# Stick-breaking attention by parts: one sigmoid, running products times differences of neighbouring value rows, with the value rows kept in DRAM

## The chip, the core and the metric

One core of a Trainium2 chip runs the whole kernel as one launch. The metric is the device time of one launch in microseconds (us); the time before is the median of three runs. A separate execution was taken by the hardware profiler, and all durations below come from it. The engines are PE (TensorE, matrix products), DVE (VectorE), ACT (ScalarE), POOL (GpSimd, which also issues DMAs from its own queue) and SP (which issues most loads).

## The reference, cut to what matters

The kernel computes one layer of a hybrid block for 1024 tokens of width 1024: a norm, one input projection, stick-breaking attention (8 heads of width 64), a gated linear recurrence (4 heads of width 128), gates, an output projection, an MLP and a last norm. The change touches only the attention:

```python
z = jnp.einsum('bhqd,bhkd->bhqk', qi, k) * scale
mask = kpos[None, :] < qpos[:, None]
log_beta = jax.nn.log_sigmoid(z)
log_rem = jnp.where(mask, log_beta - z, 0.0)
between = lax.cumsum(log_rem, axis=3, reverse=True) - log_rem
w = jnp.where(mask, jnp.exp(log_beta + between), 0.0)
return jnp.einsum('bhqk,bhkd->bhqd', w, v)
```

For a query t and a key s < t the weight is sigmoid(z_ts) times the product of sigmoid(-z_tj) over the keys j between s and t. Write R_s for the product of sigmoid(-z_tj) over s <= j < t, with R_t = 1. Because sigmoid(z) = 1 - sigmoid(-z), the weight equals R_(s+1) - R_s. Summation by parts then gives sum_s w_s v_s = sum_s (R_s - 1)(v_(s-1) - v_s), with a zero row in the place of v_(-1).

## The kernel before, in words

All matrix products are made in a split form: an operand is stored as a rounded part ("hi", type fp32r) and the remainder ("lo"). `hi_lo` (lines 152 to 154) makes both: a copy on ACT (line 144) writes hi, a subtraction on DVE (line 149) writes lo. A projection is then three matmuls per tile (`three`, line 526, all recorded at line 121).

The work is written out as one order by hand. There are two lanes of PE work (`open_block`, line 103): "main" holds the attention's own steps, "fill" holds projection steps that a `Stream` (`st`, line 471) hands out in small portions, so that PE has something to do while the other engines work on the attention. Jobs of the stream are, in order: the Q and K columns of each head (`qk_item`, line 676) and the V columns of four heads at once, a "quad" (`v_job`, line 670); behind them come projections for the recurrence. The first job (`first_job`, line 703) holds head 0's Q and K and the V columns of quad 0. The V columns of quad 1 (`v_job(1)`, line 729) stand behind head 4's Q and K. Instructions of one engine run in the order in which they stand in its queue; the tile framework places them, and lines with `after(...)` fix the order of some.

The attention is a list of 64 items (line 732): for each head the query blocks 7, 0, 6, 1, 5, 2, 4, 3 of 128 queries. The loop at line 2136 does for item i: `weights` of item i+1, `scores` of item i+2, some fill steps, `turn` of item i, and at times `values`.

- `scores` (line 736): two matmuls per 512 keys into a PSUM bank `z` (QH and QL against KS), then two sigmoids on ACT: `rm` = sigmoid(-z/8), stored one place to the left (line 755), and `bt` = sigmoid(z/8) (line 758). POOL clears the last column of `bt` (line 759).
- `weights` (line 767): a running product over `rm` from the right on DVE (line 777), which is set to 1 where the byte mask `bits` has a 1, and a product of `bt` and `rm` on DVE (line 787, recorded at line 157), 72 of each.
- `turn` (line 791): PE transposes `bt` in blocks of 128 x 128 into a bank `pw` (line 823), and `hi_lo` writes it as `wTh` and `wTl`. For an even query block POOL clears the block of keys that it doesn't reach (line 811).
- `values` (line 831): for a pair of query blocks, matmuls `po` with the V tile of each key block as weights and `wTh`, `wTl` as moving operand; ACT and DVE add the two halves of `po` into `osb` (lines 850 and 851). It runs one item behind the second `turn` of the pair.

The V tiles are made by `v_epilogue` (line 636): from a PSUM bank with 128 tokens of a quad, `hi_lo` writes hi and lo of each head side by side. `v_stat` (line 648) picks head and key block. The Q and K epilogue (line 652) writes QH, QL and KS and lets POOL issue two SBUF copies (line 663). Between them POOL issues one-time sums of output weights in DRAM (`out_weight_sums`, line 1205, issues at line 1213, tile `tw`).

On-chip buffers come from a pool of 40 full tiles of 128 x 1024 (`slot`) and 10 halves of 128 x 512 (`slot_n` up to 512 columns, `half`).

Of the kernel before, what the change touches and what calls it, by code (L numbers as in the profile page):

```python
# [19 lines left out]
P = 128  # L20
T = 1024
# [18 lines left out]
def kernel(  # L40
# [34 lines left out]
    def slot(name, dt=F32):  # L75
        return spool.tile([P, 1024], dt, tag="s", name=name)

    def slot_n(name, n, dt=F32):

        if n <= 512:  # L80
            return hpool.tile([P, 512], dt, tag="h", name=name)
        return slot(name, dt)

    def bank(name):
        return psum.tile([P, 512], F32, tag="p", name=name)
# [545 lines left out]
            )  # L631


    vt, qk, osb = {}, {}, {}

    def v_epilogue(quad):


        def ep(ps, tb):
            if tb % 2 == 0:  # L640
                vt[quad, tb // 2] = slot(f"V{quad}_{tb // 2}", F32R)
            V = vt[quad, tb // 2].rearrange("p (t h s d) -> p t h s d", t=2, h=4, s=2)
            src = ps.rearrange("p (h d) -> p h d", h=4)
            hi_lo(V[:, tb % 2, :, 0, :], V[:, tb % 2, :, 1, :], src)

        return ep

    def v_stat(h, tb):
        c = ((tb % 2) * 4 + h % 4) * P
        return vt[h // 4, tb // 2][:, c : c + P]  # L650

    def qk_epilogue(h):
        def ep(ps, half):
# [71 lines left out]
    j_qk = {0: j_first}  # L725
    for h in range(1, NHS):
        j_qk[h] = proj_jobs([qk_item(h)], xn)
        if h == 4:
            v_job(1)

    QB_ORDER = (7, 0, 6, 1, 5, 2, 4, 3)
    items = [(h, qb) for h in range(NHS) for qb in QB_ORDER]
# [3 lines left out]
    def scores(h, qb):  # L736
        open_block("main")
        nk = (qb + 1) * P
        QH, QL, KS = qk[h]
        bt, rm = slot_n(f"bt{h}_{qb}", nk), slot_n(f"rm{h}_{qb}", nk)  # L740
        step = 320 if nk == 640 else 512
        for s0 in range(0, nk, step):
            m = min(nk - s0, step)
            n = max(m, 256)
            z = bank(f"z{h}_{qb}_{s0}")
            for i, Q in enumerate((QH, QL)):
                matmul(
                    z[:, :n],
                    Q[:, qb * P : (qb + 1) * P],
                    KS[:, s0 : s0 + n],  # L750
                    start=i == 0,
                    stop=i == 1,
                )
            c0, e = int(s0 == 0), m - (s0 + m == nk)
            nc.scalar.activation(  # L755
                rm[:, s0 + c0 - 1 : s0 + m - 1], z[:, c0:m], AF.Sigmoid, scale=-0.125
            )
            nc.scalar.activation(bt[:, s0 : s0 + e], z[:, :e], AF.Sigmoid, scale=0.125)  # L758
        lastsel[0] = nc.gpsimd.memset(bt[:, nk - 1 : nk], 0.0)
        zs[h, qb] = (bt, rm)  # L760


    bits = cpool.tile([P, 1024], U8, tag="bits", name="bits")
    nc.gpsimd.memset(bits, 0)
    nc.vector.tensor_copy(bits[:, 1024 - P - 1 : 1023], ident)

    def weights(h, qb):

        nk = (qb + 1) * P
        bt, rm = zs[h, qb]
        cut = qb == NT - 1
        parts = ((512, nk - 1), (0, 512)) if cut else ((0, nk - 1),)
        for i, (a, b) in enumerate(parts):
            rr = rm[:, a:b][:, ::-1]
            sc = nc.vector.tensor_tensor_scan(  # L777
                out=rr,
                data0=rr,
                data1=bits[:, 1024 - nk + a : 1024 - nk + b][:, ::-1],  # L780
                initial=rm[:, b : b + 1] if i else 0.0,
                op0=ALU.mult,
                op1=ALU.max,
            )
            if i == 1 or (qb == 5 and h in (2,)):
                after(sc, turn_lo[0])
            m = mul(bt[:, a:b], bt[:, a:b], rm[:, a:b])
            if qb == 5:
                after(m, turn_lo[0])

    def turn(h, qb, between):

        open_block("main")
        bt, rm = zs.pop((h, qb))
# [12 lines left out]
        tiles = wTt[h, qc]  # L807
        qs = slice(par * P, (par + 1) * P)
        if par == 0:
            for t in tiles[-1]:  # L810
                after(nc.gpsimd.memset(t[:, (nkb - 1) % 4, qs].bitcast(F32), 0.0), lastsel[0])
# [341 lines left out]
    class Split:  # L1153
# [15 lines left out]

    a_sb, a_hg = Split("asb"), Split("ahg")  # L1170
    mgs = Acts("ms")
    scratch = ctx.enter_context(
        tc.tile_pool(name="scratch", bufs=1, space=bass.MemoryType.DRAM)
    )

    def dram(name, shape):
        return scratch.tile(shape, F32, tag=name, name=name)

    def half(name, dt=F32):
        return hpool.tile([P, 512], dt, tag="h", name=name)  # L1180

    def add(out, a, b):
        return nc.vector.tensor_tensor(out=out, in0=a, in1=b, op=ALU.add)

# [1102 lines left out]
```

## Time and profile before

| What | Value |
|---|---|
| time, median of 3 runs | 1452.63 us (1452.25 to 1452.66) |
| profiled execution: span from the first to the last instruction | 1450.9 us |
| the profiled execution's own time | the page gives the span only; 1.7 us lie between it and the median |
| attention in the trace | first scores at 50.11 us, last value product near 315.5 us |
| TENSOR_TENSOR_SCAN at line 777 | 72, 87.3 us in all on DVE |
| QH and QL copies issued by POOL at line 663 | 16 each, 128 KB each, 2.2 us from issue to landing |
| granted clock of PE, mean | 0.997 |

A row of a group in the profile gives the line, the engine, the operation, what it writes and reads, the count, then the busy time in us and the mean of one in ns, then the idle time of the engine just before these instructions with what ended it. A row of the windows view gives a stretch, its length, and the busy time and number of instructions of PE, of PE's weight loads (PEld), DVE, ACT and POOL, the granted clock, the busy share of the DMA engines and what they moved. In a row of the timeline the first two numbers are the start and the duration in us.

### The profile page before, as it was taken

The numbers are of one execution on the slowest core, as the hardware profiler recorded it, in microseconds if no ns is written. First come the engines' busy times: TensorE is split into PE (matmuls) and PEld (weight loads), VectorE is DVE, ScalarE is ACT, GpSimd is POOL, SyncE is SP. The second block draws the span as 40 slices with busy tenths as digits, with TensorE's granted clock in tenths as the row PEclk, the third lists the DMA queues.
The fourth block names the chain that finished last, engine by engine and source line by source line (L and its number), as shares of the span: only waits on it lengthen the run. The fifth ranks groups of instructions, "written<-read, shape, count | busy, mean of one in ns | idle before, by whom it ended". The sixth has DMA issues, their size and how long they took to land.

```text
span 1450.9 us, 19987 instructions
## 1 busy us (share of the span) xinstructions
PE 1436.3 (99%) x7470; PEld 1223.2 (84%) x7470; DVE 1100.4 (76%) x1571; ACT 668.9 (46%) x1156; POOL 143.9 (10%) x340
## 2 busy tenths in 40 slices
PE   9999999999999999999999999999999999999998
PEld 8989988988898888888877888888888888888886
DVE  6699899798746797887757898666666757768765
ACT  7566666652323243523344575444444533523443
POOL 3121121110000012100010200000000000000032
PEclk9999999999999999999999999999999999999999
DMA  7234154321303349655478414444445975676735
GB/s 211 49 97 104 37 95 81 59 44 51 102 16 102 73 142 263 226 168 177 142 219 302 162 65 147 144 159 152 152 160 185 346 272 183 250 268 251 276 102 187
DMA packets 157913, 225.73 MB, mean 156 GB/s; under 512 B 25676, under 2 KB 93816, under 8 KB 157816
## 3 DMA queue, kind: packets, MB, share of 16 engines
q1 hardware_dynamic: 142552, 183.29, 37.8%
q0 software_dynamic: 11520, 34.61, 9.6%
q10 hardware_dynamic: 3744, 6.56, 1.2%
q8 instruction: 59, 0.97, 0.3%
q14 instruction: 38, 0.31, 0.1%
HBM read 162.55 MB, written 61.87 MB: 155 GB/s over the span
## 4 chain that ended last, share of the span: by engine, by line
PE 90%; DVE 4%; issue 3%; DMA 2%; ACT 1%; POOL 1%; SPq 0%; POOLq 0%; DVEq 0%; ACTq 0%
PE pm L121 21%; PE pX L121 9%; PE pW L121 6%; PE pY L121 6%; PE pjqk L121 6%; PE pji L121 3%; PE pys L121 3%; PE pga L121 3%; PE pjg L121 2%; PE po L121 2%; PE pjv L121 2%; PE z L121 2%; PE pjf L121 2%; PE pjq L121 2%; PE gX L121 2%
## 5 line engine op out<-in xcount | busy, mean ns | idle before, releaser
L144 ACT CAST whid<-w 128x1024 fp32r<-128x1024 f32 x30 | 31.6, 1053 | 153.7 <-PE pm L121 89.5
L777 DVE TENSOR_TENSOR_SCAN rm<-rm,bits 128x511 f32<-128x511 f32 (+7 forms) x72 | 87.3, 1219 | 14.2 <-ACT rm L755 12.8
L121 PE MATMUL pm<-wlod,sh 128*128 128x512 f32 x240 | 93.5, 390 | 0.0
L121 PE MATMUL pm<-whid,sh 128*128 128x512 f32 x240 | 93.4, 389 | 0.0
L121 PE MATMUL pm<-whid,sl 128*128 128x512 f32 x240 | 93.4, 389 | 0.0
L121 PE MATMUL pm<-tl,sh 128*128 128x512 f32 (+1 forms) x210 | 81.3, 387 | 0.0
L121 PE MATMUL pm<-th,sl 128*128 128x512 f32 (+1 forms) x210 | 81.3, 387 | 0.0
L121 PE MATMUL pm<-th,sh 128*128 128x512 f32 (+1 forms) x210 | 81.3, 387 | 0.0
L149 DVE TENSOR_TENSOR wlod<-w,whid 128x1024 fp32r<-128x1024 f32 x30 | 36.6, 1221 | 53.3 <-ACT whid L144 53.2
L149 DVE TENSOR_TENSOR sl<-sa,sh 128x1024 fp32r<-128x1024 f32 x56 | 68.2, 1217 | 0.5 <-ACT sh L144 0.5
L144 ACT CAST wTh<-pw 128x128 fp32r<-128x128 f32 (+3 forms) x96 | 44.4, 487 | 50.3 <-PE pw L124 42.7
L1936 POOL TENSOR_SCALAR fss<-fss 128x1 f32<-128x1 f32 x8 | 4.5, 562 | 562.1 <-ACT fsc L1931 561.6
L144 ACT CAST sh<-sa 128x1024 fp32r<-128x1024 f32 x56 | 57.2, 1046 | 6.2 <-DMA sa<-ad 6.2
L149 DVE TENSOR_TENSOR wTl<-pw,wTh 128x512 fp32r<-128x512 f32 (+3 forms) x96 | 50.7, 547 | 8.8 <-ACT wTh L144 6.3
L121 PEld LDWEIGHTS pm<-wlod,sh 128*128 128x128 f32 x240 | 45.0, 187 | 9.9 <-DVE wlod L149 0.4
L121 PEld LDWEIGHTS pm<-whid,sh 128*128 128x128 f32 x240 | 45.1, 188 | 9.3
L121 PEld LDWEIGHTS pm<-whid,sl 128*128 128x128 f32 x240 | 45.0, 188 | 9.3
L157 DVE TENSOR_TENSOR bt<-bt,rm 128x511 f32<-128x511 f32 (+7 forms) x72 | 48.9, 685 | 5.0 <-ACT bt L758 1.0
L121 PE MATMUL pX<-sql,t1h 128*128 128x512 f32 x128 | 50.0, 391 | 0.1
L121 PE MATMUL pX<-sqh,t1l 128*128 128x512 f32 x128 | 49.8, 389 | 0.0
L121 PE MATMUL pX<-sqh,t1h 128*128 128x512 f32 x128 | 49.8, 389 | 0.0
L755 ACT ACTIVATE rm<-z 128x511 f32<-128x511 f32 (+6 forms) x96 | 47.6, 503 | 4.5 <-DVE bt L157 1.9
(923 smaller groups left out, 4598.5 us busy)
## 6 DMA issues: line engine op xcount, KB each, us to landing
w<-in_w_ff_dram SPq DMA_DIRECT2D x72, 512.0 KB, 5.4
sa<-ad SPq DMA_DIRECT2D x56, 512.0 KB, 6.6
ad<-a SPq DMA_DIRECT2D x32, 256.0 KB, 4.2
ad<-s SPq DMA_DIRECT2D x16, 512.0 KB, 5.7
tw<-in_w_out_dram POOLq DMA_DIRECT2D x24, 256.0 KB, 4.1
x<-in_x_dram SPq DMA_DIRECT2D x8, 512.0 KB, 8.6
xnl<-xnh POOLq DMA_DIRECT2D x8, 512.0 KB, 11.7
pr<-pd SPq DMA_DIRECT2D x8, 512.0 KB, 6.1
```

Of the source, the lines that this page charges most:

```text
L121: return pe(nc.tensor.matmul(*a, **k))
L144: hi_last[0] = after(in_turn("act", nc.scalar.copy(dst, src)), hi_behind[0])
L149: nc.vector.tensor_tensor(out=dst, in0=src, in1=hi.bitcast(F32), op=ALU.subtract),
L157: return nc.vector.tensor_tensor(out=out, in0=a, in1=b, op=ALU.mult)
L755: nc.scalar.activation(rm[:, s0 + c0 - 1 : s0 + m - 1], z[:, c0:m], AF.Sigmoid, scale=-0.125)
L777: sc = nc.vector.tensor_tensor_scan(out=rr, data0=rr, data1=bits[:, 1024 - nk + a : 1024 - nk + b][:, ::-1], initial=rm[:, b : b + 1] if i ...
L1936: nc.gpsimd.tensor_scalar(out=ssq, in0=ssq, scalar1=1.0 / D, scalar2=EPS, op0=ALU.mult, op1=ALU.add)
```

## The change

The weights are no longer formed. `scores` writes only `rm` = sigmoid(-z/8), unshifted; `bt`, its clearing and the product in `weights` are gone. The byte mask now has ones in all places at and above the diagonal of the last key block, so the running product is 1 there. `turn` transposes `rm`; hi is (R - 1) by an ACT activation with a bias of -1 kept in a tile of one column, lo is R - 1 minus hi in one DVE instruction.

The value rows take another way. `v_epilogue` copies two token blocks of a quad with ACT into a half tile, and POOL writes it to a DRAM tile `vrows` of 1025 rows whose row 0 is zero (`first_row`). `v_load` reads one head's 64 columns back with two DMAs on POOL's queue, once as v_s and once shifted by one row as v_(s-1); each moves 1024 rows of 64 values. `v_split` subtracts the two on DVE and makes hi and lo of the difference. Head 0's load and split stand ahead of the loop. In the loop the next head's load stands at the third of a head's eight items and its split at the sixth. `v_job(1)` moves ahead of head 4's Q and K in the stream.

```diff
-    vt, qk, osb = {}, {}, {}
+    qk, osb = {}, {}
+
+    vrows = dram("vrows", [T + 1, SBW])
+    vt, vraw = {}, {}
+
+    def first_row():
+        zero = half("vzero")[0:1, :]
+        nc.gpsimd.memset(zero, 0.0)
+        nc.gpsimd.dma_start(vrows[0:1, :], zero)
 
     def v_epilogue(quad):
+        pair = {}
+
         def ep(ps, tb):
-            if tb % 2 == 0:
-                vt[quad, tb // 2] = slot(f"V{quad}_{tb // 2}", F32R)
-            V = vt[quad, tb // 2].rearrange("p (t h s d) -> p t h s d", t=2, h=4, s=2)
-            src = ps.rearrange("p (h d) -> p h d", h=4)
-            hi_lo(V[:, tb % 2, :, 0, :], V[:, tb % 2, :, 1, :], src)
+            i, c = tb // 2, tb % 2 * 256
+            if c == 0:
+                pair[i] = half(f"v{quad}_{i}")
+            in_turn("act", nc.scalar.copy(pair[i][:, c : c + 256], ps))
+            if c:
+                rows_ = vrows[1 + i * 256 : 257 + i * 256, quad * 256 : (quad + 1) * 256]
+                nc.gpsimd.dma_start(
+                    rows_.rearrange("(t p) c -> p t c", p=P),
+                    pair.pop(i).rearrange("p (t c) -> p t c", t=2),
+                )
 
+    def v_load(h):
+        vraw[h] = slot(f"vr{h}")
+        for i, cs in halves():
+            nc.gpsimd.dma_start(
+                vraw[h][:, cs].rearrange("p (t d) -> p t d", d=DHS),
+                vrows[1 - i : T + 1 - i, h * DHS : (h + 1) * DHS].rearrange(
+                    "(t p) d -> p t d", p=P
+                ),
+            )
+
+    def v_split(h):
+        r = vraw.pop(h)
+        nc.vector.tensor_tensor(out=r[:, 0:512], in0=r[:, 512:], in1=r[:, 0:512], op=ALU.subtract)
+        vt[h] = slot(f"V{h}", F32R)
+        V = vt[h].rearrange("p (t s d) -> p t s d", s=2, d=DHS)
+        hi_lo(V[:, :, 0, :], V[:, :, 1, :], r[:, 0:512].rearrange("p (t d) -> p t d", d=DHS))
+
     def v_stat(h, tb):
-        c = ((tb % 2) * 4 + h % 4) * P
-        return vt[h // 4, tb // 2][:, c : c + P]
+        return vt[h][:, tb * P : (tb + 1) * P]
...
-        if h == 4:
-            v_job(1)
+        if h == 3:
+            j_v = v_job(1)
...
-        bt, rm = slot_n(f"bt{h}_{qb}", nk), slot_n(f"rm{h}_{qb}", nk)
+        rm = slot_n(f"rm{h}_{qb}", nk)
...
-            c0, e = int(s0 == 0), m - (s0 + m == nk)
-            nc.scalar.activation(
-                rm[:, s0 + c0 - 1 : s0 + m - 1], z[:, c0:m], AF.Sigmoid, scale=-0.125
-            )
-            nc.scalar.activation(bt[:, s0 : s0 + e], z[:, :e], AF.Sigmoid, scale=0.125)
-        lastsel[0] = nc.gpsimd.memset(bt[:, nk - 1 : nk], 0.0)
-        zs[h, qb] = (bt, rm)
+            nc.scalar.activation(rm[:, s0 : s0 + m], z[:, :m], AF.Sigmoid, scale=-0.125)
+        zs[h, qb] = rm
 
-    nc.vector.tensor_copy(bits[:, 1024 - P - 1 : 1023], ident)
+    above = slot_n("above", P)[:, 0:P]
+    nc.gpsimd.memset(above, 1.0)
+    nc.gpsimd.affine_select(
+        out=above, in_=above, pattern=[[1, P]], compare_op=ALU.is_ge, fill=0.0, base=0,
+        channel_multiplier=-1,
+    )
+    nc.gpsimd.tensor_copy(bits[:, 1024 - P :], above)
+    minus_one = cpool.tile([P, 1], F32, tag="minus_one", name="minus_one")
+    nc.gpsimd.memset(minus_one, -1.0)
 
     def weights(h, qb):
...
-        parts = ((512, nk - 1), (0, 512)) if cut else ((0, nk - 1),)
+        parts = ((512, nk), (0, 512)) if cut else ((0, nk),)
...
-            m = mul(bt[:, a:b], bt[:, a:b], rm[:, a:b])
-            if qb == 5:
-                after(m, turn_lo[0])
 
     def turn(h, qb, between):
...
-                after(nc.gpsimd.memset(t[:, (nkb - 1) % 4, qs].bitcast(F32), 0.0), lastsel[0])
+                lastsel[0] = nc.gpsimd.memset(t[:, (nkb - 1) % 4, qs].bitcast(F32), 0.0)
...
-                transpose(pw[:, kb * P : (kb + 1) * P], bt[:, s0 : s0 + P])
-            turn_lo[0] = hi_lo(
-                th[:, 0:n, qs], tl[:, 0:n, qs], pw[:, : n * P].rearrange("p (k q) -> p k q", q=P)
+                transpose(pw[:, kb * P : (kb + 1) * P], rm[:, s0 : s0 + P])
+            src = pw[:, : n * P].rearrange("p (k q) -> p k q", q=P)
+            hi_last[0] = after(
+                in_turn(
+                    "act",
+                    nc.scalar.activation(th[:, 0:n, qs], src, AF.Identity, bias=minus_one),
+                ),
+                hi_behind[0],
+            )
+            turn_lo[0] = in_turn(
+                "dve",
+                nc.vector.scalar_tensor_tensor(
+                    out=tl[:, 0:n, qs], in0=src, scalar=-1.0,
+                    in1=th[:, 0:n, qs].bitcast(F32), op0=ALU.add, op1=ALU.subtract,
+                ),
             )
...
     st.advance(11, j_qk[0])
+    first_row()
     scores(*items[0])
     weights(*items[0])
     st.advance(1, j_qk[0])
     scores(*items[1])
     st.finish(j_qk[0])
+    v_load(0)
+    v_split(0)
...
             next(wsums, None)
+        ahead = it[0] + 1
+        if ahead < NHS and i % NHS in (2, 5):
+            if ahead == NHS // 2:
+                st.finish(j_v)
+            (v_load if i % NHS == 2 else v_split)(ahead)
```

The helpers `dram` and `half`, which stood further down in the kernel, move up unchanged.

More of the change, by code (lines that the diff above doesn't have):

```diff
@@ L82, in slot_n, with dram, half @@
         return slot(name, dt)
+    scratch = ctx.enter_context(
+        tc.tile_pool(name="scratch", bufs=1, space=bass.MemoryType.DRAM)
+    )
+    def dram(name, shape):
+        return scratch.tile(shape, F32, tag=name, name=name)
+    def half(name, dt=F32):
+        return hpool.tile([P, 512], dt, tag="h", name=name)
     def bank(name):
@@ L753, in scores @@
                 )
-            c0, e = int(s0 == 0), m - (s0 + m == nk)
-            nc.scalar.activation(
-                rm[:, s0 + c0 - 1 : s0 + m - 1], z[:, c0:m], AF.Sigmoid, scale=-0.125
-            )
-            nc.scalar.activation(bt[:, s0 : s0 + e], z[:, :e], AF.Sigmoid, scale=0.125)
-        lastsel[0] = nc.gpsimd.memset(bt[:, nk - 1 : nk], 0.0)
-        zs[h, qb] = (bt, rm)
+            nc.scalar.activation(rm[:, s0 : s0 + m], z[:, :m], AF.Sigmoid, scale=-0.125)
+        zs[h, qb] = rm
     bits = cpool.tile([P, 1024], U8, tag="bits", name="bits")
     nc.gpsimd.memset(bits, 0)
-    nc.vector.tensor_copy(bits[:, 1024 - P - 1 : 1023], ident)
+    above = slot_n("above", P)[:, 0:P]
[7 more added lines that the diff above has]
+    nc.gpsimd.memset(minus_one, -1.0)
     def weights(h, qb):
         nk = (qb + 1) * P
-        bt, rm = zs[h, qb]
+        rm = zs[h, qb]
         cut = qb == NT - 1
-        parts = ((512, nk - 1), (0, 512)) if cut else ((0, nk - 1),)
+        parts = ((512, nk), (0, 512)) if cut else ((0, nk),)
         for i, (a, b) in enumerate(parts):
@@ L786, in weights @@
                 after(sc, turn_lo[0])
-            m = mul(bt[:, a:b], bt[:, a:b], rm[:, a:b])
-            if qb == 5:
-                after(m, turn_lo[0])
     def turn(h, qb, between):
         open_block("main")
-        bt, rm = zs.pop((h, qb))
+        rm = zs.pop((h, qb))
         qc, par = qb // 2, qb % 2
@@ L822, in turn @@
                 s0 = (4 * i + kb) * P
-                transpose(pw[:, kb * P : (kb + 1) * P], bt[:, s0 : s0 + P])
-            turn_lo[0] = hi_lo(
-                th[:, 0:n, qs], tl[:, 0:n, qs], pw[:, : n * P].rearrange("p (k q) -> p k q", q=P)
+                transpose(pw[:, kb * P : (kb + 1) * P], rm[:, s0 : s0 + P])
[6 more added lines that the diff above has]
+                hi_behind[0],
+            )
+            turn_lo[0] = in_turn(
[4 more added lines that the diff above has]
+                ),
             )
@@ L1171 @@
     mgs = Acts("ms")
[L1172 to L1180, printed above, removed]
     def add(out, a, b):
```

## The prediction

> **What bounds the kernel now.** I read first the engine table and the chain of the page, then PE's waits over the whole trace, then the busy time by stretch.
>
> ```profile
> span 1450.9 us, 19987 instructions
> PE 1436.3 (99%) x7470; PEld 1223.2 (84%) x7470; DVE 1100.4 (76%) x1571; ACT 668.9 (46%) x1156; POOL 143.9 (10%) x340
> ...
> PE 90%; DVE 4%; issue 3%; DMA 2%; ACT 1%; POOL 1%; SPq 0%; POOLq 0%; DVEq 0%; ACTq 0%
> ```
>
> The chain that ended last is 90% PE, and PE is idle for 1450.9 - 1436.3 = 14.6 us only. Where is that idle time? PE's waits answer:
>
> ```profile
> engine line waited for: us in total, times, longest us
> PE pwW L121 <- DVE h L1186: 4.5, 1, 4.5
> PE warm L121 <- POOL ident masks.py:199: 2.2, 1, 2.2
> PE sl L121 <- DVE q L157: 0.2, 1, 0.2
> ```
>
> One wait lies at the very start and one in the output projection; none belongs to the attention. The windows confirm it (columns: stretch, length, PE, PEld, DVE, ACT, POOL busy, granted clock, DMA share, GB/s):
>
> ```profile
> core 0: us, PE busy (x) PEld busy (x) DVE busy (x) ACT busy (x) POOL busy (x), PEclk, DMA share, GB/s
> 52.00:316.00 264.00, 263.83 (x1680) 237.14 (x1679) 234.40 (x334) 171.45 (x397) 49.83 (x183) 1.00 0.34 72
> 700.00:770.00 70.00, 65.42 (x276) 53.25 (x275) 42.46 (x60) 24.95 (x33) 8.94 (x14) 0.95 0.70 214
> 1100.00:1400.00 300.00, 300.00 (x1325) 248.41 (x1324) 205.41 (x212) 116.17 (x132) 0.99 (x3) 1.00 0.68 245
> ```
>
> From 52 to 316 us, the stretch that the change rewrites, PE lacks 0.17 us of being always busy, at full granted clock. DVE is busy 234.40 / 264 = 89%, ACT 65%, POOL 19%. So DVE is close to being the limit there, but it is not: the projection steps that are laid between the items keep PE supplied. The other engines can end earlier without anybody waiting for them.
>
> **The change part by part.** PE's work first: the matmuls of `scores`, the 288 transposes (of `rm` in place of `bt`) and the 320 of `values` stay as they are in number and shape. Nothing is taken off the bound.
>
> What goes and what comes on the other engines:
>
> ```profile
> L157 DVE TENSOR_TENSOR bt<-bt,rm 128x511 f32<-128x511 f32 (+7 forms) x72 | 48.9, 685 | 5.0 <-ACT bt L758 1.0 <-issue 0.2
> L758 ACT ACTIVATE bt<-z 128x383 f32<-128x383 f32 (+5 forms) x96 | 47.8, 506 | 1.0 <-PE po L121 1.0
> L759 POOL MEMSET bt<- 128x1 f32 x64 | 6.8, 124 | 77.9 <-PE po L121 38.6 <-PE pw L124 14.8 <-DVE wTl L149 7.2
> L149 DVE TENSOR_TENSOR V<-pjv,V x16: 397/416/424, 18.9 to 161.9; 128x256 fp32r<-128x256 f32 x16
> L149 DVE TENSOR_TENSOR wTl<-pw,wTh 128x512 fp32r<-128x512 f32 x48 | 32.6, 682 | 8.7 <-ACT wTh L144 6.3 <-PE pw L124 2.0
> L325 DVE SCALAR_TENSOR_TENSOR xnl<-xnt,prm,xnh 128x512 fp32r<-128x512 f32 x8 | 5.3, 732 | 0.0
> L144 ACT CAST wTh<-pw 128x512 fp32r<-128x512 f32 x48 | 28.3, 591 | 35.4 <-PE pw L124 28.4 <-issue 3.7 <-DVE bt L157 2.9
> L1288 ACT ACTIVATE g<-pga,prm x8: 680/682/707, 365.4 to 560.8; 128x512 f32<-128x512 f32 x8
> ```
>
> DVE loses the 72 products (48.9 us) and the 16 V remainders (16 x 0.416 = 6.7). It gains two operations of 128 x 512 per head, a subtraction and a remainder: 8 x (0.69 + 0.68) = 11.0, with 0.685 and 0.682 from the rows of `bt` and `wTl`. The remainder of the weights becomes a three-operand instruction; `xnl` is the same instruction from PSUM, 0.732 against 0.682, so 96 x 0.05 = 4.8 at most. Sum for DVE: 11.0 + 4.8 - 48.9 - 6.7 = -39.8 us, 89% down to about 74% of the stretch. ACT loses 47.8 us of sigmoids, gains 8 hi copies (8 x 0.59 = 4.7) and pays more for the hi of the weights, which now takes its bias from a column: `g` at line 1288 is such an activation from PSUM, 0.682 against 0.591, so 96 x 0.09 = 8.7. Sum -34 us. The V copies on ACT stay. [...] All of this lies beside PE's projection steps. Its worth on the path is the idle time that PE has there: at most 0.17 us. If that cover were gone, it would be worth up to 40 us; 263.83 of 264 says that it is not.
>
> At the start POOL builds the new mask: two memsets, an affine select, a conversion, while DVE loses one conversion. POOL does such a piece in 0.3 us and is idle for 3 us before it is first needed:
>
> ```profile
> 1.90 0.29 POOL masks.py:199 TENSOR_SCALAR_AFFINE_SELECT ident<-ident 128x128 f32<-128x128 f32 x1
> ...
> 5.39 0.19 POOL L609 TENSOR_TENSOR n_ms<-n_ms,n_ss 128x1 f32<-128x1 f32 x1 [3.04 <-ACT n1scr L604]
> ```
>
> Four pieces of 0.3 are 1.2 us, under 3.04: nothing. `v_job(1)` ahead of head 4's Q and K: the same steps in another order; 44 steps instead of 53 lie before its end, and it ends several items before head 3's third item needs it. Nothing.
>
> What is new is the way of V through DRAM, and the one place where it is short of time is head 0. The rows:
>
> ```profile
> 52.34 0.28 PE L121 MATMUL pjv<-wv0h,xnl 128*128 128x256 f32 x1
> 54.03 0.41 ACT L144 CAST V<-pjv 128x256 fp32r<-128x256 f32 x1
> 69.05 0.36 PE L121 MATMUL po<-wTh,V 128*128 128x256 f32 x1
> fd<-yr POOLq DMA_DIRECT2D x12, 256.0 KB, 3.0
> wqk1r<-in_w_in_dram SPq DMA_DIRECT2D x2, 256.0 KB, 4.3
> L663 POOL DMA_DIRECT2D QL<-QL x16: 516/516/531, 31.6 to 219.7; - x16
> L1213 POOL DMA_DIRECT2D tw<-in_w_out_dram x24: 523/547/983, 44.6 to 237.5; - x24
> ```
>
> The last V copy of quad 0 ends at 54.4 us (perhaps 1 us earlier, since two sigmoids ahead of it are gone). POOL then writes the last 256 KB; the write of `yr` to DRAM from the same queue lands 3.0 us after its issue: 57.4. POOL issues the two loads. No row shows POOL issuing 1024 rows. QL has 64 rows (0.516) and tw 128 (0.547), so a row costs 0.5 ns and an issue of 1024 about 0.52 + 0.47 = 1.0 us; if instead each row cost QL's whole 0.516 / 64 = 8 ns, it would be 8.3 us. I take 1.0, by the slope of these two rows, and keep 8.3. The second issue then starts at 58.4. Its landing: `wqk1r` is the same shape from DRAM (1024 rows of 64 values), on another queue, 4.3 us: 62.7. Then subtraction, hi copy and remainder, 0.69 + 0.59 + 0.68 = 2.0: head 0's V stands at 64.7, and `po` first needs it at 69.05. Cover 4.3 us, cost 0. With issues of 8.3 us the loads would land near 57.4 + 16.6 + 3.8 = 77.8 and V stand at 79.8: 10.7 us late. From an issue of about 3.2 us on the cover is used up.
>
> [...]
>
> For the later heads the load is issued three items before the split, and the split stands six items before the first use. An item takes 264 / 64 = 4.1 us, so the cover is 12 and 25 us. Behind a waiting load on POOL's queue stand the QH and QL copies of the next heads, the clearing of `wTh` and `wTl` and the weight sums; behind a waiting `v_split` on DVE stand the running products. These are the rivals.
>
> Sum: 0 to -0.17 us on PE, 0 for head 0, 0 for the rest: span 1450.8, and with the 1.7 us between span and median 1452.6, no change.
>
> **The rivals.** First, POOL's queue becomes late (slower). Place: the two loads stand in one queue with the clearing that `po` waits for and with QH and QL; head 0's V needs both of them. For it: today a clearing ends just before its use:
>
> ```profile
> 90.37 0.22 POOL L811 MEMSET wTl<- 128x128 f32 x1
> 90.65 0.36 PE L121 MATMUL po<-wTh,V 128*128 128x256 f32 x1
> ```
>
> Against it: the stretch leaves POOL idle for 81%, and 64 clearings with their waits on buffers go away. Price: with an issue of 3 us the two hold POOL for 6, against the item of 4.1 that lies between load and first use of the clearing: about 2 us for each of 7 heads, 14 us at most if none of it is hidden. With 5 us head 0 alone is late by 57.4 + 10 + 3.8 + 2.0 - 69.05 = 4.2. It decides from an issue of about 2.5 to 3 us on, and gives 1456 to 1467. Chance 0.22.
>
> Second, DVE waits in its own queue (slower). Its order is fixed before the run: if head 0's split is placed as if the rows came sooner than they do, the running products behind it wait too.
>
> ```profile
> 53.72 1.22 DVE L777 TENSOR_TENSOR_SCAN rm<-rm,bits 128x511 f32<-128x511 f32 x1 [4.02 <-ACT rm L755]
> 55.65 1.28 DVE L777 TENSOR_TENSOR_SCAN rm<-rm,bits 128x512 f32<-128x512 f32 x1
> 57.76 2.33 DVE L777 TENSOR_TENSOR_SCAN rm<-rm,bits 128x127 f32<-128x127 f32 x2
> ```
>
> The first three items' running products take 1.22, 1.28 and 2.33 us; without the multiplications and V remainders between them they end near 53.7 + 4.9 = 58.6, and the rows land at 62.7: 4 us of waiting, 1456.7 if PE has none of it covered. Against it: DVE's own saving of 40 us over the stretch gives it back, and the transpositions have some us of cover. Chance 0.06.
>
> Third, PE has slack that its busy time hides (faster). The first matmul after a block of transpositions is longer than its sister of the same shape:
>
> ```profile
> L121 PE MATMUL z<-KS,QH 128*128 128x512 f32 x40 | 17.0, 426 | 0.0
> L121 PE MATMUL z<-KS,QL 128*128 128x512 f32 x40 | 15.7, 393 | 0.0
> L121 PE MATMUL po<-wTh,V 128*128 128x256 f32 x160 | 42.4, 299 | 0.1
> L121 PE MATMUL po<-wTl,V 128*128 128x256 f32 x160 | 39.7, 283 | 0.0
> ```
>
> If these were short waits for ACT or DVE, 40 x 0.033 + 160 x 0.016 = 3.9 us would come back, with the 0.17 about 4: 1448.5. Against it: it happens at every change of kind, whatever the load on DVE. [...] Chance 0.06.
>
> Fourth, the hand-over at 763 us moves. Buffers are handed out in another order, and PE's one long wait depends on when a load of `h` can start:
>
> ```profile
> 763.39 0.80 PE L121 MATMUL pwW<-wout21h,msh 128*128 128x512 f32 x1 [4.53 <-DVE h L1186]
> L121 PE MATMUL pwW<-wout21h,msh 128*128 128x512 f32 x16 | 7.6, 475 | 4.5 <-DVE h L1186 4.5
> h<-in_x_dram POOLq DMA_DIRECT2D x4, 512.0 KB, 9.7
> ```
>
> After the wait of 4.53 us the granted clock of that window is 0.95 and matmuls that take 389 elsewhere average 475 ns: up to 48 x 0.086 = 4.1 us more. So the place is worth 4.5 + 4.1 = 8.6 us at most in gain, and a later load would cost as much per us. For it: buffer turns are reshuffled. Against it: the 400 us between hold the same work. Chance 0.06, half to each side.
>
> **How the numbers follow.** About 0.2%, 2.9 us, is what a measurement can tell from no change. Forecast (no change) 0.60; POOL's queue late 0.22; DVE's 0.06; hidden slack 0.06; hand-over 0.03 faster, 0.03 slower. So faster 0.09, same 0.60, slower 0.31. The predicted time is that of the forecast, 1452.6. Range: the low end is the forecast's own edge, 1449.7, leaving out most of the 0.09; the high end goes into the first rival to 1461, two thirds of its prices, leaving out about 0.1.
>
> **What would show it.** Right: PE's busy time in 52 to 316 us as now, DVE there near 195 us, the loads of `vr` issued in about 1 us and landing in 4 to 6, no PE wait at the first `po`. Wrong: PE waiting on `V`, `wTh` or `rm` near 60 to 70 us, POOL's issues of `vr` above 3 us, or a wait at `pwW` that isn't 4.5 us. A gain with PE's attention matmuls unchanged in length would contradict the bound itself.

## The result, and the profile after

The changed kernel takes 1460.09 us (median of 4 runs, 1459.23 to 1461.57), the kernel before, measured beside it, 1452.64: ratio 1.0054, interval [1.0040, 1.0069]. It is 7.5 us slower; no change was forecast. The profiled executions have spans of 1458.7 and 1450.9 us, 7.8 apart.

The head of the page of the changed kernel, as at the start of the prediction:

```profile
span 1458.7 us, 19714 instructions
PE 1438.6 (99%) x7470; PEld 1224.4 (84%) x7470; DVE 1060.9 (73%) x1498; ACT 645.8 (44%) x1068; POOL 164.1 (11%) x306
```

DVE is 39.5 us less busy and ACT 23.1, and nobody has gained by it: PE still does the same 7470 matmuls. PE's idle time grew from 14.6 to 20.1 us and its busy time by 2.3, together the 7.8. Its waits over the whole trace say where:

```profile
PE pwW L131 <- DVE h L1229: 4.5, 1, 4.5
PE po L131 <- DVE wTl L875: 3.0, 3, 1.6
PE warm L131 <- POOL ident masks.py:199: 2.3, 1, 2.3
PE gX L131 <- DVE gu L1226: 1.1, 1, 1.1
PE pjqk L131 <- DVE xnl L335: 0.7, 1, 0.7
PE po L131 <- ACT wTh L869: 0.6, 1, 0.6
PE z L131 <- ACT rm L795: 0.5, 1, 0.5
```

The wait at `pwW` is unchanged, and so is `warm`. The others are new: `pjqk` lies at the start, `z` and `po` in the attention, `gX` behind it. None of those in the attention names V, `vr` or POOL. The windows of the changed kernel, with the columns of the prediction's, show the place:

```profile
52.00:316.00 264.00, 259.85 (x1641) 232.69 (x1640) 192.14 (x261) 144.09 (x301) 66.17 (x146) 0.99 0.42 92
58.00:74.00 16.00, 14.61 (x83) 12.04 (x82) 11.21 (x15) 9.24 (x18) 5.71 (x13) 1.00 0.46 123
104.00:111.00 7.00, 4.74 (x22) 4.09 (x21) 6.67 (x9) 5.13 (x10) 2.44 (x6) 0.76 0.25 53
700.00:770.00 70.00, 65.12 (x286) 53.24 (x285) 43.92 (x62) 24.87 (x34) 8.92 (x14) 1.00 0.62 180
```

From 52 to 316 us PE now lacks 4.15 us of being always busy, where it lacked 0.17. Two short stretches hold most of it: 1.39 us between 58 and 74, 2.26 between 104 and 111. In the second the granted clock is 0.76 on the mean.

Operations that both kernels have make a useful ruler. The copy `ot<-po` closes each block of `values`, 32 times; start of the first and of the last, first before, then after:

```profile
L850 ACT COPY ot<-po x32: 363/368/372, 71.2 to 315.8; 64x256 f32<-64x256 f32 x32
```

```profile
L903 ACT COPY ot<-po x32: 363/368/371, 74.1 to 322.6; 64x256 f32<-64x256 f32 x32
```

The first is 2.8 us later, the last 6.8. So 6.8 of the 7.8 us are lost by the end of the attention; the wait at `gX`, at 738.7 us, is part of the rest. In the timeline of ACT the fifth copy starts at 104.83 before and at 111.33 after: 6.5 us of the 6.8 are lost by then. There are two places, and a small one ahead of them.

**Near 102 us.** ACT's timeline in the changed kernel (start, duration, in brackets the idle time before and who ended it):

```profile
97.79 0.37 ACT L869 ACTIVATE wTh<-pw,minus_one 128x128 fp32r<-128x128 f32 x1 [2.15 <-PE pw L134]
102.26 1.05 ACT L154 CAST wqk4h<-wqk4r 128x1024 fp32r<-128x1024 f32 x1 [4.10 <-DMA wqk4r<-in_w_in_dram]
103.21 0.86 ACT L795 ACTIVATE rm<-z 128x512 f32<-128x512 f32 x2
```

The hi copy of head 4's weights waits 4.10 us for its load. Behind it in ACT's queue stand two sigmoids whose inputs are long there: PE's last matmul of that `z` (the first row of PE's fence below) ended at 98.4. In these rows ACT takes its instructions in the order of its queue: the sigmoids start at 103.21, 4.8 us after their input ended and 0.95 us after the copy. The wait travels on: DVE's running product stands idle for the sigmoids, and PE for what comes of it. DVE's row, then PE's:

```profile
104.11 1.76 DVE L821 TENSOR_TENSOR_SCAN rm<-rm,bits 128x768 f32<-128x768 f32 x1 [5.63 <-ACT rm L795]
```

```profile
98.17 0.27 PE L131 MATMUL z<-KS,QL 128*128 128x256 f32 x1
...
105.92 0.38 PE L131 MATMUL po<-wTh,V 128*128 128x256 f32 x1 [0.64 <-ACT wTh L869]
107.92 0.58 PE L131 MATMUL po<-wTl,V 128*128 128x256 f32 x1 [1.61 <-DVE wTl L875]
108.30 0.42 PE L131 MATMUL po<-wTh,V 128*128 128x256 f32 x1
108.52 0.41 PE L131 MATMUL po<-wTl,V 128*128 128x256 f32 x1
```

The last two rows are 0.22 us apart; such matmuls at 93.79 and 93.91 us are 0.12 apart. A mean clock of 0.76 over 7 us is, as an estimate, a half clock for 7 x 0.24 / 0.5 = 3.4 us. A window inside that stretch shows the half itself:

```profile
109.00:110.00 1.00, 1.00 (x6) 1.00 (x6) 1.00 (x3) 0.21 (x1) 0.49 (x1) 0.50 0.47 102
```

Why is the load late? SP's timeline, after and then before:

```profile
94.19 1.12 SPq L139 DMA_DIRECT2D wqk4r<-in_w_in_dram  x2
```

```profile
44.92 1.09 SPq L129 DMA_DIRECT2D wqk4r<-in_w_in_dram  x2
```

`v_job(1)` now comes ahead of head 4's Q and K, so its two raw pieces take both buffers of the tag `raw`, and `wqk4r` is issued 49 us later, when they come free. Before, the hi copy ran at 84.81 and waited for no load.

**Near 63 us.** ACT's timeline at head 0, after, and PE's waits there:

```profile
60.66 0.38 ACT L795 ACTIVATE rm<-z 128x256 f32<-128x256 f32 x1 [7.10 <-PE z L131]
63.26 0.62 ACT L154 CAST V<-vr 128x512 fp32r<-128x512 f32 x1 [2.22 <-DVE vr L685]
63.79 0.97 ACT L795 ACTIVATE rm<-z 128x512 f32<-128x512 f32 x2
```

```profile
64.43 0.38 PE L131 MATMUL z<-KS,QH 128*128 128x256 f32 x1 [0.48 <-ACT rm L795]
71.91 0.38 PE L131 MATMUL po<-wTl,V 128*128 128x256 f32 x1 [0.91 <-DVE wTl L875]
```

It is the same pattern. The hi copy of head 0's V waits 2.22 us for the subtraction, and through it for the rows from DRAM; the third item's sigmoids (63.79) stand behind it. PE had ended their `z` at 54.0. They are nearly 10 us late because two instructions stand ahead of them on ACT: the fourth item's sigmoid, which waits 7.10 us for its own `z`, and the copy of V. PE's row, then DVE's:

```profile
53.68 0.34 PE L131 MATMUL z<-KS,QL 128*128 128x384 f32 x1
```

```profile
63.91 0.69 DVE L159 TENSOR_TENSOR V<-vr,V 128x512 fp32r<-128x512 f32 x1 [0.69 <-ACT V L154]
64.79 2.02 DVE L821 TENSOR_TENSOR_SCAN rm<-rm,bits 128x896 f32<-128x896 f32 x1 [0.19 <-ACT rm L795]
```

DVE's queue has the same fault: V's remainder stands ahead of that item's running product and ends at 64.60, so the product could have started only 0.19 us sooner had the sigmoids been in time.

**At the start.** POOL's timeline, then ACT's, after:

```profile
2.79 0.76 POOL L1256 DMA_DIRECT2D tw<-in_w_out_dram  x1
```

```profile
9.16 1.14 ACT L154 CAST wqk0whi<-wqk0r 128x512 fp32r<-128x512 f32 x2 [2.56 <-DMA wqk0r<-in_w_in_dram]
```

The weight sums' first load ran at 44.6 us before. It is ordered behind `lastsel[0]`, which was a memset of `bt`; that memset is gone, the variable is still empty when the first load is made, and nothing holds it. It runs beside `wqk0r`, whose first hi copy starts at 9.16 instead of 7.2. PE's first `pjqk` starts at 11.55 against 10.75; 0.34 us of that stays (the last matmul of `pjv` at 52.68 against 52.34).

### The profile page after: what moved, and what is told of

It reads as the page before. It is cut to its first block, busy times and chain, and to the rows that moved or that the text cites. A ratio compares the mean times of both kernels' runs of the same rounds, so it can differ in the third digit from the quotient of the medians.

```text
span 1458.7 us, 19714 instructions
## 1 busy us (share of the span) xinstructions
PE 1438.6 (99%) x7470; PEld 1224.4 (84%) x7470; DVE 1060.9 (73%) x1498; ACT 645.8 (44%) x1068; POOL 164.1 (11%) x306
## 5 line engine op out<-in xcount | busy, mean ns | idle before, releaser
L821 DVE TENSOR_TENSOR_SCAN rm<-rm,bits 128x512 f32<-128x512 f32 (+6 forms) x72 | 87.2, 1222 | 27.3 <-ACT rm L795 26.9
L875 DVE SCALAR_TENSOR_TENSOR wTl<-pw,wTh 128x512 fp32r<-128x512 f32 (+2 forms) x96 | 50.6, 549 | 38.8 <-ACT wTh L869 38.5
L869 ACT ACTIVATE wTh<-pw,minus_one 128x512 fp32r<-128x512 f32 (+2 forms) x96 | 53.1, 581 | 45.0 <-PE pw L134 43.4
L795 ACT ACTIVATE rm<-z 128x512 f32<-128x512 f32 (+3 forms) x96 | 43.6, 489 | 8.6 <-PE z L131 7.5
L131 PEld LDWEIGHTS pm<-tl,sh 128*128 128x128 f32 x210 | 39.5, 188 | 8.1
```

The costliest lines, as they stand in the source:

```text
L131: return pe(nc.tensor.matmul(*a, **k))
L795: nc.scalar.activation(rm[:, s0 : s0 + m], z[:, :m], AF.Sigmoid, scale=-0.125)
L821: sc = nc.vector.tensor_tensor_scan(out=rr, data0=rr, data1=bits[:, 1024 - nk + a : 1024 - nk + b][:, ::-1], initial=rm[:, b : b + 1] if i ...
L869: nc.scalar.activation(th[:, 0:n, qs], src, AF.Identity, bias=minus_one),
L875: nc.vector.scalar_tensor_tensor(out=tl[:, 0:n, qs], in0=src, scalar=-1.0, in1=th[:, 0:n, qs].bitcast(F32), op0=ALU.add, op1=ALU.subtract,),
```

## The experiments

Theory A: two loads head ACT's queue, and all behind them waits; the work itself costs nothing. Theory B: the `vr` loads slow the weight loads, wherever they meet. Theory C: the new weights are slower on the way from `pw` to `po`. Ratios are to the kernel before, measured beside each run. "First" and "last" are the starts of the first and last `ot`, 71.2 and 315.8 us before, 74.1 and 322.6 after.

**v_job(1) back at its place**

```diff
-        if h == 3:
+        if h == 4:
             j_v = v_job(1)
```

> Theory A (ACT's queue behind a late load): with v_job(1) behind head 4's Q and K again, wqk4r gets its raw buffer some 50 us earlier, the hi copy wqk4h waits for nothing, the sigmoids behind it are in time, and the 4.1 us of PE's lag at 102 to 111 us go: 1456 us. What remains is the 2 us at 63 to 72 us, 0.4 at the start and 1 later. Theory B (the vr loads slow the weight loads down): the order of the jobs does not matter, wqk4r or another weight load lands as late as before beside the vr loads, 1460 us. Theory C (the new remainder and bias of the weights lie on the way from pw to po): 1460 us.

1454.45 us, ratio 1.0027 [1.0018, 1.0036]; last 319.1. The order of the jobs is about half of the loss, as A said.

**Head 0's split later**

```diff
     v_load(0)
-    v_split(0)
...
+        if i == 1:
+            v_split(0)
         if i % 2 == 1:
             next(wsums, None)
```

> Only head 0's split moves, from ahead of the first item into the second one, so that two more items' sigmoids stand ahead of its hi copy on ACT. Theory A: the z matmul no longer waits for rm at 64 us, the lag of 2 us at 63 to 72 us goes, the wait at 102 us stays: 1458 us. If the split comes too late for the first po, PE waits there for V instead and nothing is gained. Theory B and C: 1460 us.

1457.99 us, ratio 1.0044 [1.0032, 1.0057]; first 71.7 instead of 74.1, last 320.7. PE no longer waits at 64 and 72 us, and `po` does not wait for V. The third item's sigmoids have ended by 54.75 now (ACT's next row, at 60.04, stands behind 5.29 us of idle time), and its running product lies ahead of the split. The edit moves the split on both engines, so it doesn't tell ACT's queue and DVE's apart.

**The kernel before with the order alone**

```diff
-        if h == 4:
+        if h == 3:
             v_job(1)
```

> The kernel before with one edit alone: v_job(1) ahead of head 4's Q and K. No value rows in DRAM, the old weights. Theory A: wv1r holds both raw buffers here too, wqk4r is issued near 94 us, its hi copy waits on ACT near 100 us; this kernel has no vr load beside it, so the wait may be 2 us and not 4, but the time rises: 1454.5 to 1457 us. Theory B and C: 1452.6 us, no change.

1453.16 us, ratio 1.0008 [0.9999, 1.0017]; last 317.1. It costs less than A said. The answer for the tile `wqk4r`:

```profile
L129 SPq DMA_DIRECT2D wqk4r<-in_w_in_dram x2: 368/476/584, 93.9 to 94.3; - x2
L144 ACT CAST wqk4h<-wqk4r x1: 1056/1056/1056, 98.7 to 98.7; 128x1024 fp32r<-128x1024 f32 x1
...
DMA to landing us min/median/max: 3.3/3.8/4.4
```

The load is as late as in the changed kernel, but it lands in 3.8 us, not 7.2, and the hi copy stands behind the item's sigmoids, not ahead of them. So a late load alone does little; its place in the queue and its landing have to be told apart. Why the copy stands ahead of the sigmoids in the changed kernel and behind them here was not examined.

**The new weights alone.** V is made on the chip as before, so the differences of neighbouring values are left out of the computation; `v_job(1)` is at its old place.

> The new weights (running products alone, one column longer, hi with a bias of -1, three-operand remainder) with V made on the chip as in the kernel before and v_job(1) at its old place. The differences of neighbouring values are left out of the computation. Theory A: the arithmetic costs PE nothing, 1452.6 us, within 1 us. Theory B: the same, 1452.6. Theory C: 1457 to 1460 us, with PE waiting for wTl or wTh several times between 60 and 316 us.

1451.83 us, ratio 1.0006 [0.9997, 1.0014]; last 315.8. Theory C falls.

**Both orders mended** (the first two edits together)

> The changed kernel with v_job(1) behind head 4's Q and K again and head 0's split in the second item. Theory A: the two waits at the head of ACT's queue are all but some 1 us of the loss, so the two gains add up: from the kernel before 0 to +2 us, ratio 1.000 to 1.0015, and PE's lag stays under 1 us up to 150 us. Theory B (weight loads slowed by the vr loads wherever they meet): a ratio of about 1.003, other weight loads are late in place of wqk4r.

1452.27 us, ratio 1.0012 [1.0004, 1.0021]; first 71.6, last 317.9. The two gains add up.

**Only the hi copy's place**

```diff
             if nxt:
+                hi_behind[0] = qh.get((3, 1)) if nxt[0].name == "wqk4" else hi_behind[0]
                 nxt[0].split()
```

`qh` keeps the QH copies of `qk_epilogue`; (3, 1) is head 3's last.

> The changed kernel, jobs and loads as they are; one order on ACT's queue only: the hi copy wqk4h stands behind the last QH copy of head 3 and no longer ahead of two sigmoids. wqk4r is issued as late as before and lands as slowly. Theory A: the sigmoids, the running product and the weights of that item are in time, the 4.1 us at 102 to 111 us go, with the half clock that followed them: ratio to the kernel before about 1.0027. Theory B: the late landing itself is what PE waits for, 1.0054.

1453.36 us, ratio 1.0016 [1.0007, 1.0024]; last 318.0. The tile `wqk4r` in this kernel:

```profile
L154 ACT CAST wqk4h<-wqk4r x1: 1053/1053/1053, 106.1 to 106.1; 128x1024 fp32r<-128x1024 f32 x1
...
DMA to landing us min/median/max: 6.3/6.7/7.1
```

Load and landing are as late as ever, the copy runs at 106.1, later than in the changed kernel, the sigmoids run at 97.78, and the loss at 102 us is gone: PE is busy for all of the 7 us from 104 to 111. PE did not need these weights, its first matmul with them comes at 149.3 us in the changed kernel; it needed the sigmoids behind them. This is the mechanism, and B's first form falls. The gain is more than expected: `last` comes 4.6 us earlier, the fall of the ratio is worth 5.5 us, and what lies between isn't placed.

**Head 2's vr loads two items earlier**

```diff
+        at = 0 if ahead == 2 else 2
-        if ahead < NHS and i % NHS in (2, 5):
+        if ahead < NHS and i % NHS in (at, 5):
```

> The changed kernel, only head 2's two vr loads are issued two items earlier, so that they have landed before wqk4r is issued. The hi copy keeps its place ahead of the sigmoids. If the vr loads doubled wqk4r's landing (7.2 us against 3.8 us with the same order in the kernel before), it lands in about 4 us, ACT's wait shrinks from 4.1 to about 0.7 us and the lag at 102 to 111 us by about 3 us: ratio about 1.003. If the landing is slow for another cause (tw, or wv1's end), it stays at 7 us and the ratio at 1.0054.

1454.75 us, ratio 1.0026 [1.0017, 1.0035]; last 319.3.

```profile
its engine sat idle before it (us, times) until:
  DMA wqk4r<-in_w_in_dram: 2.5, 1
...
DMA to landing us min/median/max: 5.2/5.6/5.9
```

The landing falls from 7.2 to 5.6 and ACT's wait from 4.1 to 2.5: the `vr` loads are 1.6 us of the slow landing. What the rest is was not tried. B holds as a part: the slow landing lengthens the wait at the head of the queue.

**wv1r into buffers of its own**

```diff
         unit = v_unit(quad)
+        unit.roomy = (0, 1)
```

> The changed kernel with its order of jobs, but wv1r lands in two full buffers of the general pool in place of the two raw buffers, so that wqk4r can be loaded 45 us earlier. Theory A: not the order but the raw buffers made wqk4r late; the wait of 4.1 us on ACT is gone, ratio about 1.0027. If the order itself costs (the V job's own copies and splits at another time), the ratio stays above 1.004.

1454.84 us, ratio 1.0019 [1.0011, 1.0028]; last 318.2. `wqk4r` is issued at 45.4 again and the hi copy runs at 86.9, although the order of the jobs is the new one. It was the two raw buffers.

**Three orders mended:** the split later, the hi copy's place, and the first `tw` load behind the first value row

```diff
-        nc.gpsimd.dma_start(vrows[0:1, :], zero)
+        lastsel[0] = nc.gpsimd.dma_start(vrows[0:1, :], zero)
```

> Three orders of the changed kernel together, its work and its jobs as they are: head 0's split in the second item, wqk4h behind head 3's last QH copy, and the first tw load behind the clearing of the first value row (in the changed kernel nothing holds that load, and it starts at 2.8 us, beside wqk0r). If the loss is orders alone, PE's lag against the kernel before stays under 0.6 us up to 160 us and the ratio is 0.999 to 1.001. If the route of V or the new weights cost something by themselves, the ratio stays above 1.002.

1453.43 us, ratio 1.0013 [1.0004, 1.0021]; first 71.0, last 315.8. In the attention the loss is gone; the total stays a little above what was expected, a miss by 0.3 thousandths. The single gains of the three edits (1.0, 3.8 and 1.0 thousandths) add up to more than the 4.1 measured together; with intervals of about one thousandth to each side they still agree.

**The same with every vr load issued twice**

> The same, with every vr load issued twice: 1.8 us more of POOL's queue and 512 KB more traffic for each of eight heads. Rival of POOL's queue: each of seven heads is late by up to 1.8 us, up to 12 us in all, ratio 1.004 to 1.009. Theory A (POOL has cover, only what heads ACT's and DVE's queue counts): at most 1 us more than without the doubling, most likely at head 0, ratio 0.999 to 1.002.

1458.86 us, ratio 1.0052 [1.0039, 1.0064]: a miss for theory A, and inside the range of the rival of POOL's queue. First 73.5 (2.5 later than without the doubling), last 319.0 (3.2 later), in the fastest of its runs. POOL and DVE at head 0:

```profile
60.05 0.88 POOL L680 DMA_DIRECT2D vr<-vrows  x1 [1.87 <-DMA vr<-vrows]
61.27 0.88 POOL L680 DMA_DIRECT2D vr<-vrows  x1 [0.34 <-DMA vr<-vrows]
```

```profile
65.36 0.69 DVE L689 TENSOR_TENSOR vr<-vr 128x512 f32<-128x512 f32 x1 [1.76 <-DMA vr<-vrows]
```

The second load into the same buffer waits on POOL for 1.87 us, until the first has landed, and the subtraction starts at 65.36, 2.8 us later than in the changed kernel. Head 0 pays; the other seven heads together pay 0.7 us in this trace, most of it a wait of 0.55 us at 82 us for a QL copy that stands behind head 1's loads in POOL's queue. So in this execution POOL has cover behind head 0, and head 0 has next to none left. The median lies 3 us above the profiled run; what the other executions pay, and whether POOL's queue is in it, isn't settled.

**The first tw load alone**

> The changed kernel with one edit: the first tw load waits for the clearing of the first value row. wqk0r lands near 7 us as in the kernel before, PE's lag at 50 us falls from 0.34 us to about 0.1, the rest stays: ratio about 1.005. If the new mask pieces on POOL made the start late, the lag stays 0.34.

1457.55 us, ratio 1.0044 [1.0032, 1.0057]. The hi copy `wqk0whi` starts at 7.2 again and PE no longer waits at `pjqk`; the rest stays. The trace shows 0.4 us; that the median fell by more is within the intervals.

**Three orders, wqk4r loaded early in place of the moved copy**

> Head 0's split in the second item and the first tw load later as in the run with three orders, but wqk4r loaded early into its own buffer (wv1r in two full buffers) in place of the moved hi copy. Ratio 0.999 to 1.001 as well, if the order on ACT's queue is all that the late load cost.

1453.39 us, ratio 1.0014 [1.0005, 1.0023]; last 315.8, as with the moved copy, and again a little above what was expected.

The next four ask where the last 1.3 thousandths are.

**Three orders, vr loads issued by SP**

```diff
-            nc.gpsimd.dma_start(
+            nc.sync.dma_start(
                 vraw[h][:, cs].rearrange("p (t d) -> p t d", d=DHS),
```

> The kernel with three orders mended, the vr loads issued by SP and no longer by POOL. If the rest of the loss (ratio 1.0013) is POOL's queue, it goes: 0.999 to 1.0005. If it is the traffic or the hand-over at 763 us, it stays: 1.001 to 1.002.

1451.90 us, ratio 1.0007 [0.9999, 1.0016]; last 315.8. Between the two expectations, and the interval overlaps that of the loads on POOL.

**The new weights alone, the first tw load late** (V's differences left out again)

> The new weights alone with V made on the chip (the differences are left out of the computation), the first tw load behind head 0's copies of Q. If the rest of the loss belongs to the route of V, 0.9995 to 1.0005; if it belongs to the new weights, about 1.001.

1451.10 us, ratio 0.9999 [0.9991, 1.0008]; last 314.9. The arithmetic is free; the rest belongs to V's route or to the hand-over behind it.

**The kernel before, again**

> The kernel before, unchanged: ratio 0.9992 to 1.0008. Its trace on this chip is what the lags of the other runs of this call are measured against.

1450.95 us, ratio 1.0001 [0.9993, 1.0010]; last 315.0.

**The changed kernel, again**

> The changed kernel, unchanged: ratio 1.004 to 1.0065 as at first, with the waits at 64, 72, 102 and 108 us and the half clock behind the last.

1459.72 us, ratio 1.0063 [1.0051, 1.0075]; first 73.5, last 321.0. The waits are there again, but without the half clock at 108 us.

What remains with three orders mended is for the most part not in the attention: `last` is 315.8 with the loads on POOL and on SP alike, and 315.8 and 315.0 in the two profiles of the kernel before, so by the profiles at most 0.8 us of it lies there. The profiles differ at the hand-over near 763 us. Windows of the kernel with the loads on POOL, with the loads on SP, and of the kernel before, repeated:

```profile
700.00:790.00 90.00, 84.21 (x362) 68.92 (x361) 60.06 (x78) 34.91 (x43) 8.98 (x14) 0.96 0.72 223
```

```profile
700.00:790.00 90.00, 87.37 (x383) 71.32 (x383) 61.56 (x79) 36.03 (x44) 8.94 (x14) 1.00 0.74 231
```

```profile
700.00:790.00 90.00, 85.96 (x373) 70.63 (x372) 61.64 (x80) 36.07 (x44) 8.93 (x14) 0.98 0.71 226
```

In one profile each, PE does 362, 383 and 373 matmuls in the same 90 us, at a granted clock of 0.96, 1.00 and 0.98. From the last `ot` to the last `pwW` the three take 455.8, 450.9 and 453.7 us. These are single executions, and the kernel before itself took 455.7 us in its first profile. The granted clocks of all runs say a little more: with the loads on POOL the mean clock was 0.996 in 7 of 11 runs, in the kernel before beside it in 3 of 22 (one of 1885 us left out); with the loads on SP in 2 of 12 against 2 of 29. So with the loads on POOL the clock is lower on the average. It isn't all: at a mean clock of 0.997 three runs of that kernel take 1453.9 us on the mean and 14 of the kernel before 1451.8. Where those runs lose it stays open; a version that beats the kernel before was not found.

## Why the prediction was wrong

**The step that failed** reads: "`v_job(1)` ahead of head 4's Q and K: the same steps in another order ... Nothing." The steps on PE are the same. But a job also takes buffers for its loads one job ahead, and a V job takes two raw buffers where a Q/K job takes one. That moved `wqk4r` by 49 us, put its hi copy at the head of ACT's queue without data, and cost 3.7 us by the ruler (fifth `ot` 6.5 late, first 2.8), the half clock included. Moving the hi copy alone brings the ratio from 1.0054 to 1.0016. The order has this price only together with the rest of the change: in the kernel before its ratio is 1.0008 [0.9999, 1.0017], with the copy behind the sigmoids and the load landing in 3.8 us. The prediction counted 44 steps against 53; it did not follow the loads that are issued with them.

**Head 0's chain** was right in every time and wrong in who waits. Forecast were two issues of 1.0 us, landing 62.7, V ready at 64.7, `po` at 69.05:

```profile
L676 POOL DMA_DIRECT2D vr<-vrows x16: 889/924/1575, 56.6 to 263.6; - x16
L685 DVE TENSOR_TENSOR vr<-vr x8: 659/666/693, 62.5 to 270.8; 128x512 f32<-128x512 f32 x8
L154 ACT CAST V<-vr x8: 611/620/640, 63.3 to 279.2; 128x512 fp32r<-128x512 f32 x8
L159 DVE TENSOR_TENSOR V<-vr,V x8: 673/683/693, 63.9 to 279.9; 128x512 fp32r<-128x512 f32 x8
```

Issues of 0.92, subtraction at 62.5, V ready at 63.9 + 0.69 = 64.6. `po` never waits for V. The step "Cover 4.3 us, cost 0" set V against its own reader only. The hi copy is also an instruction in ACT's queue and the remainder one in DVE's, and for what stands behind them there was no cover: 2.0 us by the matmuls that both kernels have. The prediction's own sign of being wrong came, PE waiting on `rm` at 64 us. (Its edge of 3.2 us for an issue comes out at 2.9 by the sum that it uses for 5 us: (69.05 - 57.4 - 3.8 - 2.0) / 2.)

The landing of 4.3 us, taken from `wqk1r`, came out at a median of 5.1 for `vr` (3.8 to 7.5). In the trace before, the loads of that shape for which the DMA view gives a landing (`wqk1r` to `wqk3r`, `wqk5r`, `wqk6r`) have medians of 3.4 to 4.4.

**The start**, "nothing": the four mask pieces did fit. Missed was that the removed memset was what the first `tw` load was ordered behind, 0.4 us.

**The bound** was right: PE, and less work on DVE and ACT is worth nothing. The new weights alone, with the first `tw` load late, give 0.9999.

**The sizes.** DVE's sum was forecast at -39.8 and came out at 1060.9 - 1100.4 = -39.5, but by luck. These rows of the changed kernel, and `wTl` and `wTh` before with 547 and 487 ns, show that the third operand costs 2 ns each and not 50 (the groups that went and came add up to -48.9 - 6.7 + 5.5 + 5.4 = -44.7, more than the engine's busy time fell):

```profile
L875 DVE SCALAR_TENSOR_TENSOR wTl<-pw,wTh 128x512 fp32r<-128x512 f32 (+2 forms) x96 | 50.6, 549 | 38.8 <-ACT wTh L869 38.5
```

```profile
L869 ACT ACTIVATE wTh<-pw,minus_one 128x512 fp32r<-128x512 f32 (+2 forms) x96 | 53.1, 581 | 45.0 <-PE pw L134 43.4
```

The bias column costs 94 ns each, as forecast (8.7 us). ACT's busy time fell by 23.1 and not 34: sigmoids in a row overlap (in the kernel before with the order alone, two of 0.60 and 0.59 us start 0.50 apart). Removing 96 of them frees 96 x 0.1 = 9.6 us less than their durations, 34 - 9.6 = 24, an estimate. A column of the running product takes 2.1 ns (1.74 us for 768 columns at 69.54 us, 0.94 for 384 at 72.25); 72 more are 0.15 us.

**The range and the rivals.** The measured time lies inside the stated range of 1449.7 to 1461 by luck: the range reached that far for a late queue of POOL, and that was not the cause. POOL's queue: wrong for the changed kernel, the issue takes 0.92, not 3 us, and PE waits for nothing of POOL's in the attention. DVE in its own queue at head 0: the nearest, right in place and kind, twice too large (4 us said, 2.0 measured). The wait that ended last there was ACT's, by 0.19 us, and no run parts the two; that ACT's queue would hold up the sigmoids, at head 0 and at 102 us, no rival had. Hidden slack: the new weights alone, at 0.9999, show none. The longer first matmul stands behind transposes outside the attention too (`pwY` 0.47 us at 819.65 in the kernel before, against 0.39), but not at every change of kind: `pjqk` behind `z` at 60.12 us takes 0.39 there, as its sisters do. Hand-over: the wait at `pwW` stayed 4.5 us; over all profiles the way from the last `ot` to the last `pwW` takes 450.9 to 456.2 us, a spread as large as most gains here.

## What to carry to other kernels

When an order changes, list the loads and buffers that come with each step, not only its work on the bound engine: here a load that slipped by 49 us put a copy that waited 4.10 us at the head of a queue, and the price was what stood behind it, not what read it. So ask of every instruction that waits for a DMA what is queued behind it on its engine, and put it late if its reader can wait; here one such copy was worth 0.4%. When an instruction is removed, look for what was ordered behind it.

## What the runs showed of the hardware

In some executions the granted clock falls to one half at a short stall of PE. In the changed kernel it is 0.75, 0.50, 0.50 and 0.55 in the four windows of 1 us from 107 to 111 us, together 3.4 us of half clock; it begins near 107.5, and PE's wait ends at 107.92. In the first profile of the kernel before it is 0.73 from 762 to 763 us, 0.50 up to 769 and 0.86 in the next, together 6.8 us; PE's wait ends there at 763.39.

Near 105 us PE was idle for 2.26 us in two waits, and the half clock came with them in the first trace of the changed kernel. It did not when that kernel was run again, though PE was idle for 2.52 us there in the same stretch:

```profile
104.00:111.00 7.00, 4.48 (x33) 3.91 (x32) 6.91 (x10) 6.12 (x13) 2.44 (x6) 1.00 0.26 56
```

So in these two traces the longer idle time is the one without the half clock; what decides was not shown. At 763 us the half clock came in all 13 profiles in which PE waits once, for 3.6 to 5.2 us: the longest weight load of `pwW` takes 329 to 338 ns there, at a median of 187 or 188. In the five in which PE waits twice, for 2.6 us at most at a time, the longest takes 189. The mean clock of 700 to 790 us was read in eight of the 18 profiles: it is 0.98 or 0.96 in six of the 13, an estimate of 3.6 or 7.2 us of half clock, and 1.00 in two of the five. Why PE waits there once in some executions and twice in others was not tried.
